# A decoder layer on one core: the last norm's weights on ScalarE, x2 in steps of 704 columns, and four steps moved ahead of others

## The chip, the cores and the metric

One core of a Trainium2 chip runs the whole kernel. The metric is the device time of one execution in microseconds (us). TensorE multiplies, VectorE and ScalarE do elementwise work, GpSimd does additions in SBUF, and SyncE (SP) issues the DMAs.

## The reference

One decoder layer for 1024 prompt tokens and 8 x 4 sample tokens (1056 columns), all in float32. Cut to what this change touches:

```python
def _rms(x, g):
    y = x * lax.rsqrt(jnp.mean(x * x, axis=-1, keepdims=True) + EPS)
    return y * g

a, k_state, v_state = attn_fn(q, k, v)        # sliding window for the prompt, cache for the samples
...
mix = concatenate([a, m]) @ w_out
x = x + _rms(mix, n_mix_post)
f = _rms(x, n_ffn_pre)
f = (silu(f @ w_gate) * (f @ w_up)) @ w_down
x = x + _rms(f, n_ffn_post)                                  # the last norm: weights gn[:, 3, :] in the kernel
x = x + sigmoid(x @ w_ple_gate) * (p @ w_ple)                # the embedding, with its gate
```

## The kernel before

Features lie on the partitions, tokens on the columns. The 1056 tokens are three groups (0, 1, 2) of 352 columns, and a tensor of 1024 features for one group is eight tiles of 128 x 352, kept as two halves of four tiles (128 x 1408). A product in float32 precision is three matmuls: each operand is split into a rounded part and a remainder (`split`: a cast on ScalarE, L164, then a subtraction on VectorE, L165), and `gemm` issues high x high, high x low and low x high, all on L126. Weights come from DRAM by SP into three raw buffers and are split ahead of their use. `weights(j, ahead)` and `need(k, ahead)` do this, as far ahead as their argument says.

A PSUM tile takes one of eight banks (`bank`), handed out in turn; a matmul into a bank waits for the last reader of the tile that had it before.

The stages, in order: the input norm and projection, the pooling mixer, the attention, the output projection with its norms, eleven slabs of the feed-forward part, and the embedding.

*Attention.* The sample queries are done between the prompt's blocks: `dscores`, then `dturned` twice (eight transposes and one more, copied to SBUF by ScalarE, L747 and L750), then `dvalues`, which multiplies the transposed weights with the cached values. The prompt's eight blocks follow in the order 6, 7, 5, 0, 1, 2, 3, 4: while one block is turned and multiplied, the next one's `scores` are computed. `filler` puts output products between them. Masks are multiplied in `turned` on VectorE, L687 and L689. The weights of the output projection come through `weights`, the last of them in `out_proj`.

*Feed-forward.* Gate and up products of groups 0 and 1 go through sums of weights, which GpSimd makes in four additions of 128 x 512 each (L980), after which ScalarE and VectorE split them (`sh`, `sl`). `hid_put` splits the product of the two (L165, `hid`). `down` multiplies `hid` with the down weights and adds each tile of 128 x 352 to `o` in SBUF (L1077).

*Last norm and embedding.* Group 2 is done with its slabs earlier than groups 0 and 1, so its last norm runs under their slabs. `last_down` is `down` and a Square of the finished tile on ScalarE (L779 for the first, L782), which VectorE sums in `acc` (L783). `ple_steps` is the rest of the norm: loads and split of p, loads of the residual into x2, `rstd_steps` (a matmul with ones, the square root on ScalarE, L302, and on VectorE reciprocal, split and two diagonals `dg`, L310, which two matmuls spread over the partitions as r in a PSUM bank), then for each half y times r (L1107) and, tile by tile, x2 plus y times weight (L1111), and `f_operand`, the split of x2 (cast `fh`, remainder `fl`). `ple_out` computes one output tile: the embedding product (pp, 6 matmuls), the gate product (pg, 24 matmuls), the sigmoid (L1155), and the product and the sum on VectorE (L1157, L1159).

`chain` and `turn` interleave such steps with the matmuls: a generator yields its estimated load on VectorE and a delay, and `turn(n)`, called after n matmuls, resumes it when its time has come. The program's order on each engine comes from there and from a scheduler behind it; `behind` keeps group 2's steps in the order of the program.

Of the kernel before, what the change touches and what calls it, by code (L numbers as in the profile page):

```python
# [12 lines left out]
AF = mybir.ActivationFunctionType  # L13
ALU = mybir.AluOpType
AX = mybir.AxisListType

P = 128
D = 1024
KC = D // P
# [6 lines left out]
N = T // G  # L26
NS = (N,) * G
OFF = tuple(N * g for g in range(G + 1))
# [33 lines left out]
def trunk_kernel(  # L62
# [31 lines left out]
    nc = tc.nc  # L94
    te, ve, se, ge = nc.tensor, nc.vector, nc.scalar, nc.gpsimd
# [14 lines left out]
    def act_tile(shape, dt=F32, s="a"):  # L110
        return apool.tile(shape, dt, tag="a", bufs=A_SLOTS, name=nm(s))
# [21 lines left out]
    def tmp(n, s="t", dt=F32):  # L133
        return spool.tile([P, n], dt, tag="tmp", bufs=6, name=nm(s), padded_shape=[P, NX])
# [7 lines left out]
    gn = const([P, 4, KC], gains)  # L142
# [20 lines left out]
    def split(hi, lo, src):  # L163
        fix(se.copy(hi, src))  # L164
        fix(ve.tensor_tensor(lo, src, hi.bitcast(F32), op=ALU.subtract))  # L165
# [23 lines left out]
    def weights(j, ahead=W_PAIRS - 1):  # L189
        for i in range(j, j + ahead + 1):  # L190
            w_split(i)
            w_load(i + 1)
        return pairs[j]
# [10 lines left out]
    WOA, WO = [[], []], [[None] * 4, [None] * 4]  # L204
# [19 lines left out]
    for s, gs in WALK:  # L224
        pairs_of = []
        for i in range(SLAB):
            c = SLAB * s + i
# [48 lines left out]
    def gemm(ps, ops, start=True, stop=True):  # L276

        last = len(ops) - 1
        for i, (wh, wl, xh, xl) in enumerate(ops):
            mm(ps, wh, xh, start=start and i == 0, stop=False)  # L280
            mm(ps, wh, xl, start=False, stop=False)
            mm(ps, wl, xh, start=False, stop=stop and i == last)
# [52 lines left out]
    def bc4(r):  # L335
        return r.unsqueeze(1).to_broadcast([P, 4, r.shape[1]])
# [311 lines left out]
    def scores(b):  # L648


        t = act_tile([P, 8, WIN])
        cur = [bank() for _ in range(2)]
        prv = [bank() for _ in range(2)] if b else None
        for c in range(4):
            for which, at in ((cur, b), (prv, b - 1)):
                if which is None:
                    continue
                for kv in range(2):
                    rows = slice(64 * kv, 64 * kv + 64)
                    mm(  # L660
                        which[kv][:, c * WIN : (c + 1) * WIN],
                        qT[c][rows, b * WIN : (b + 1) * WIN],
                        kT[rows, at * WIN : (at + 1) * WIN],
                        start=True,
                        stop=True,
                    )
        for kv in range(2):
            tk = t[:, 4 * kv : 4 * kv + 4, :]
            if b:
                se.copy(tk, v4(prv[kv]))  # L670
                ve.copy_predicated(tk, m4(0).bitcast(mybir.dt.int32), v4(cur[kv]))  # L671
            else:
                ve.tensor_tensor(tk, v4(cur[kv]), m4(1), op=ALU.add)
            hs = slice(4 * kv, 4 * kv + 4)
            softmax(tk, 4, 0.125, skp[:, hs], nskp[:, hs])
        return t

    def turned(b, t):

        ptc = act_tile([P, 8, WIN])  # L680
        ptp = act_tile([P, 8, WIN]) if b else None
        for kv in range(2):
            ps = bank()
            hs = slice(4 * kv, 4 * kv + 4)
            for c in range(4):
                mt(ps[:, c * P : (c + 1) * P], t[:, 4 * kv + c, :])
            ve.tensor_tensor(ptc[:, hs, :], v4(ps), m4(2), op=ALU.mult)  # L687
            if b:
                ve.tensor_tensor(ptp[:, hs, :], v4(ps), m4(3), op=ALU.mult)  # L689
        return ptc, ptp  # L690
# [62 lines left out]
    def dvalues(pts, o):  # L753

        sides = [slice(64 * kv, 64 * kv + 64) for kv in range(2)]

        def own(a, b):
            return a.rearrange("p (h r) -> p h r", h=4)[:, :, DSEQ * b : DSEQ * (b + 1)]

        for pt, cols in zip(pts, sides):  # L760
            mm(o[cols, :P], vdec[:, cols], pt[: NDEC * DSEQ, 8, :], start=True, stop=False)
        for b in range(NDEC):
            for pt, cols in zip(pts, sides):
                mm(own(o[cols, :P], b), cvt[:, b, cols], own(pt[:, b, :], b), start=False, stop=b == NDEC - 1)
# [12 lines left out]
    def squares_into(acc_g, src, first):  # L777
        if first:
            se.activation(acc_g, src, AF.Square)  # L779
        else:  # L780
            sq = tmp(src.shape[-1], "sq")
            se.activation(sq, src, AF.Square)  # L782
            ve.tensor_tensor(acc_g, acc_g, sq, op=ALU.add)  # L783
# [10 lines left out]
        se.activation(yv, yv, AF.Identity, scale=gn[:, 1, m : m + 1])  # L794

    def out_proj(m, g):
        w = weights(WO[g != 2][m], int(g == 2))
        ps = bank()
        if ys[g][1] is None:
            ys[g][1] = half(g, s="y")  # L800
        gemm(ps[:, : NS[g]], ops8(w, [mixa[g], mixp[g]]))
        se.activation(ys[g][1][:, m - 4, :], ps[:, : NS[g]], AF.Identity, scale=gn[:, 1, m : m + 1])
        squares_into(acc[g], ps[:, : NS[g]], False)
# [9 lines left out]
    def filler(n):  # L813
        for _ in range(n):
            if fill:
                f, *at = fill.pop(0)
                f(*at)
# [4 lines left out]
    t = scores(order[0])  # L822
# [4 lines left out]
    filler(1)  # L827
    pts.append(dturned(td[1]))
    filler(1)
    dvalues(pts, od)  # L830
    put(od, SEQ, NDEC * DSEQ)
    kse = act_tile([P, NDEC, WIN])
# [3 lines left out]
    nc.scalar.dma_start(vs_o, cvt[DSEQ:, :, :])  # L836
    nc.scalar.dma_start(vn_o, vdec)
    for a, b in zip(order, order[1:] + [None]):
        t2 = None if b is None else scores(b)
        filler(1)  # L840
        parts = turned(a, t)
        filler(1)
        values(a, parts)
        t = t2
# [19 lines left out]
    def turn(n):  # L864

        now[0] += n
        for ch in [ch for ch in chains if ch[2]] or list(chains):
            while ch in chains and ch[1] <= now[0]:
                try:
                    load, wait = next(ch[0])  # L870
                except StopIteration:
                    chains.remove(ch)
                    break
                dve[0] = max(dve[0], now[0]) + load / share[0]
                ch[1] = dve[0] + wait
# [46 lines left out]
    def f_operand(src, g):  # L922
        hi, lo = half(g, F32R, "fh"), half(g, F32R, "fl")
        split(hi, lo, src)
        return hi, lo
# [159 lines left out]
    def last_down(n, m, g):  # L1085
        down(n, m, g)
        if m == 0:
            acc3[g] = acc_tile(g)
        squares_into(acc3[g], os_[g][m // 4][:, m % 4, :], m == 0)

    def ple_steps(g):

        pl = half(g, F32R, "pl")
        pls[g] = pl[:, 0:2, :], pl[:, 2:4, :]
        for k in range(2):
            pr = tmp(NS[g], "pr")
            nc.sync.dma_start(pr, p[:, k, OFF[g] : OFF[g + 1]])
            split(pl[:, k, :], pl[:, 2 + k, :], pr)
        x2s[g] = []
        for h in range(2):  # L1100
            x2[g][h] = half(g, s="x2")
            nc.sync.dma_start(x2[g][h], x1d[g][h])
        r = yield from rstd_steps(acc3[g])
        behind = tc.keep_in_program_order if g == 2 else lambda ins: ins
        for h in range(2):
            yh, xh = os_[g][h], x2[g][h]
            behind(ve.tensor_tensor(yh, yh, bc4(r), op=ALU.mult))  # L1107
            for c in range(4):
                k = 4 * h + c
                behind(  # L1110
                    ve.scalar_tensor_tensor(  # L1111
                        xh[:, c, :], yh[:, c, :], gn[:, 3, k : k + 1], xh[:, c, :], op0=ALU.mult, op1=ALU.add
                    )
                )
                if g == 2 and c % 2:
                    yield 6, 0
            yield 12 if g == 2 else 24, 0
            x2s[g].append(f_operand(xh, g))
            yield 10, 0

    END = len(WALK) - 1

# [22 lines left out]
    def ple_out(n, m, g):  # L1145
        ph, pl = pls[g]
        w = WPE[n][m]
        wh, wl = need(w[0])
        cols = slice((m % 4) * P, (m % 4 + 1) * P)
        pp, pg = bank(), bank()  # L1150
        gemm(pp[:, :N], [(wh[:, k, cols], wl[:, k, cols], ph[:, k, :], pl[:, k, :]) for k in range(2)])
        gemm(pg[:, :N], ops8(need(w[1]), x2s[g]))
        turn(30)
        sg = tmp(N, "sg")
        se.activation(sg, pg[:, :N], AF.Sigmoid)  # L1155
        xm = x2[g][m // 4][:, m % 4, :]
        ve.tensor_tensor(sg, sg, pp[:, :N], op=ALU.mult)  # L1157
        yo = tmp(N, "yo")
        ve.tensor_tensor(yo, sg, xm, op=ALU.add)  # L1159
        nc.sync.dma_start(y_o[:, m, OFF[g] : OFF[g + 1]], yo)  # L1160
# [105 lines left out]
```

## Time and profile before

| | |
|---|---|
| median of three runs | 1124.63 us (1122.67 to 1124.66) |
| the profiled execution | 1121.84 us, its span 1120.1 us |
| granted clock of TensorE in the profiled execution | 0.997 |
| VectorE, ScalarE, GpSimd busy | 748.4, 440.7, 179.5 us |
| HBM read and written | 88.30 and 10.11 MB |
| DMA of p (176 KB) and of x2 (704 KB), issue to landing | 2.7 and 6.2 us |

The span is the time from the first to the last instruction in the trace. A time such as 868.51 is counted from its start. PE is TensorE, DVE VectorE, ACT ScalarE, POOL GpSimd. In a row, `out<-in` gives the program's names of the tiles without their numbers, and a line number belongs to the kernel before. Matmuls overlap, so the length of one (0.32 us for 352 columns) is twice the distance to the next.

### The profile page before, as it was taken

To read this page: it belongs to the slowest core of one execution; us is meant where nothing else is said; L and a number is where in the kernel's file an instruction comes from. 1 tells how busy PE (TensorE), PEld (TensorE's weight loads), DVE (VectorE), ACT (ScalarE), POOL (GpSimd) and SP (SyncE) were. 2 spreads that over 40 slices of the span, in tenths; PEclk is the share of its full clock that TensorE was granted. 3 is DMA by queue.
4 is the path that set the end of the run, shared out by engine and by line. 5 is a ranking of instruction groups with operands and counts; after the bars stand their busy time and mean duration, and the time that the engine had idled before them with its cause. 6 is when DMAs were issued, how large, how long until landed. Compare 5 with 4: busy or idle time off the path is not lost.

```text
span 1120.1 us, 17702 instructions
## 1 busy us (share of the span) xinstructions
PE 1108.9 (99%) x7171; PEld 1090.8 (97%) x7171; DVE 748.4 (67%) x1244; ACT 440.7 (39%) x782; POOL 179.5 (16%) x152
## 2 busy tenths in 40 slices
PE   8999999999999999999999999999999999999998
PEld 8999988899999999999999999999999999999998
DVE  6667468985879955355554555557887877789532
ACT  8323276664646524331321314124424334366220
POOL 0045132200000041011111101111132123100000
PEclk9999999999999999999999999999999999999999
DMA  8121311272543312111110212112212222246211
GB/s 288 57 70 43 119 41 38 83 265 71 206 159 132 114 38 76 39 61 54 38 57 20 75 38 76 39 39 93 104 57 77 74 76 79 96 161 215 91 58 39
DMA packets 35265, 99.54 MB, mean 89 GB/s; under 512 B 4180, under 2 KB 14708, under 8 KB 35184
## 3 DMA queue, kind: packets, MB, share of 16 engines
q1 hardware_dynamic: 33856, 96.65, 25.6%
q10 hardware_dynamic: 1328, 1.77, 0.5%
q8 instruction: 56, 0.92, 0.4%
q14 instruction: 25, 0.20, 0.1%
HBM read 88.30 MB, written 10.11 MB: 88 GB/s over the span
## 4 chain that ended last, share of the span: by engine, by line
PE 88%; DVE 6%; ACT 3%; DMA 1%; issue 1%; POOL 0%; SPq 0%; DVEq 0%; ACTq 0%; POOLq 0%
PE b L126 88%; ACT a L634 1%; DVE wl L165 1%; DMA xr<-in_x_dram 1%; DVE mx L626 1%; DVE a L671 1%; ACT wh L164 1%; POOL wr L980 0%; DVE h L366 0%; PE b L120 0%; DMA c<-in_gains_dram 0%; DVE o L1107 0%; DVE x L1111 0%; DVE a L734 0%; DVE p L1014 0%
## 5 line engine op out<-in xcount | busy, mean ns | idle before, releaser
L126 PE MATMUL b<-fh,wh 128*128 128x352 f32 x808 | 260.7, 323 | 0.0
L126 PE MATMUL b<-fh,wl 128*128 128x352 f32 x808 | 259.3, 321 | 0.0
L126 PE MATMUL b<-fl,wh 128*128 128x352 f32 x808 | 259.0, 321 | 0.0
L126 PE MATMUL b<-hid,wh 128*128 128x352 f32 x1056 | 252.5, 322 | 1.7 <-DVE o L1107 1.2
L164 ACT CAST wh<-wr 128x1024 fp32r<-128x1024 f32 (+1 forms) x139 | 142.9, 1030 | 249.6 <-PE b L126 206.6
L165 DVE TENSOR_TENSOR wl<-wr,wh 128x1024 fp32r<-128x1024 f32 (+1 forms) x139 | 171.7, 1238 | 63.8 <-ACT wh L164 63.6
L126 PEld LDWEIGHTS b<-hid,wh 128*128 128x128 f32 x1056 | 182.3, 188 | 2.5 <-issue 1.5
L126 PE MATMUL b<-hid,wl 128*128 128x352 f32 x528 | 169.0, 320 | 0.0
L980 POOL TENSOR_TENSOR wr<-wr 128x512 f32<-128x512 f32 x44 | 63.4, 1441 | 622.3 <-DVE wl L165 451.8
L126 PEld LDWEIGHTS b<-fl,wh 128*128 128x128 f32 x808 | 151.8, 188 | 0.0
L126 PEld LDWEIGHTS b<-fh,wl 128*128 128x128 f32 x808 | 151.8, 188 | 0.0
L126 PEld LDWEIGHTS b<-fh,wh 128*128 128x128 f32 x808 | 151.6, 188 | 0.0
L1077 DVE TENSOR_TENSOR o<-o,b 128x352 f32<-128x352 f32 x240 | 114.7, 514 | 27.3 <-PE b L126 27.2
L126 PE MATMUL b<-fh,sh 128*128 128x352 f32 x352 | 113.6, 323 | 0.0
L126 PE MATMUL b<-fl,sh 128*128 128x352 f32 x352 | 112.8, 320 | 0.0
L126 PE MATMUL b<-fh,sl 128*128 128x352 f32 x352 | 112.7, 320 | 0.0
L126 PE MATMUL b<-h,wh 128*128 128x352 f32 x480 | 106.1, 327 | 1.3 <-ACT h L364 0.9
L165 DVE TENSOR_TENSOR sl<-wr,sh 128x1024 fp32r<-128x1024 f32 x44 | 53.7, 1222 | 75.5 <-ACT sh L164 75.5
L126 PEld LDWEIGHTS b<-hid,wl 128*128 128x128 f32 x528 | 99.0, 187 | 0.0
L164 ACT CAST sh<-wr 128x1024 fp32r<-128x1024 f32 x44 | 45.7, 1047 | 130.9 <-POOL wr L980 91.3
L126 PEld LDWEIGHTS b<-h,wh 128*128 128x128 f32 x480 | 82.6, 190 | 2.6 <-DVE h L366 1.3
L126 PE MATMUL b<-h,wl 128*128 128x352 f32 x240 | 66.3, 325 | 0.0
(150 smaller groups left out, 1593.3 us busy)
## 6 DMA issues: line engine op xcount, KB each, us to landing
wr<-in_w_gu_dram SPq DMA_DIRECT2D x64, 512.0 KB, 3.3
wr<-in_w_dn_dram SPq DMA_DIRECT2D x32, 512.0 KB, 3.5
wr<-in_w_pg_dram SPq DMA_DIRECT2D x14, 512.0 KB, 3.7
x<-in_x_dram SPq DMA_DIRECT2D x6, 704.0 KB, 7.7
x1d<-x SPq DMA_DIRECT2D x6, 704.0 KB, 3.5
x<-x1d SPq DMA_DIRECT2D x6, 704.0 KB, 6.2
out_y_dram<-yo SPq DMA_DIRECT2D x24, 176.0 KB, 1.8
wr<-in_w_out_b_dram SPq DMA_DIRECT2D x8, 512.0 KB, 3.3
```

The lines of the kernel that those rows point to most:

```text
L126: ins = te.matmul(*args, **kw)
L164: fix(se.copy(hi, src))
L165: fix(ve.tensor_tensor(lo, src, hi.bitcast(F32), op=ALU.subtract))
L626: ve.tensor_reduce(mx, t, axis=AX.X, op=ALU.max)
L634: se.activation(t[:, c, :], t[:, c, :], AF.Exp, bias=nmx[:, c : c + 1], scale=scale, accum_out=sm[:, c : c + 1])
L671: ve.copy_predicated(tk, m4(0).bitcast(mybir.dt.int32), v4(cur[kv]))
L980: ge.tensor_tensor(out, a, b, op=op)
L1077: ve.tensor_tensor(o, o, v, op=ALU.add)
```

## The change

Five things are edited. In `last_down` the weight of the last norm is multiplied into the tile by ScalarE (an Identity with a scale, in place, after the Square). In `ple_steps` p comes in one DMA into a buffer of the activation pool, the loads are issued first, y times r and x2 plus y are done in steps of two tiles (704 columns) without the weight, and the split of p comes last. In `ple_out` the gate product is ahead of the embedding product, and the sigmoid is between them. In the attention the scores of the second block are ahead of `dvalues`. For the last block the split of the first weight of the output projection for groups 0 and 1 is called for behind `turned`, and `out_proj` fetches one weight less ahead at its end.

```diff
     def out_proj(m, g):
-        w = weights(WO[g != 2][m], int(g == 2))
+        w = weights(WO[g != 2][m], int(g == 2 and m < KC - 1))
...
     pts.append(dturned(td[1]))
     filler(1)
+    ahead = scores(order[1])
     dvalues(pts, od)
     put(od, SEQ, NDEC * DSEQ)
...
     for a, b in zip(order, order[1:] + [None]):
-        t2 = None if b is None else scores(b)
+        t2 = ahead or (None if b is None else scores(b))
+        ahead = None
         filler(1)
         parts = turned(a, t)
+        if b is None:
+            weights(WOA[1][0], 1)
         filler(1)
...
     def last_down(n, m, g):
-        squares_into(acc3[g], os_[g][m // 4][:, m % 4, :], m == 0)
+        o = os_[g][m // 4][:, m % 4, :]
+        squares_into(acc3[g], o, m == 0)
+        se.activation(o, o, AF.Identity, scale=gn[:, 3, m : m + 1])
 
     def ple_steps(g):
         pl = half(g, F32R, "pl")
         pls[g] = pl[:, 0:2, :], pl[:, 2:4, :]
-        for k in range(2):
-            pr = tmp(NS[g], "pr")
-            nc.sync.dma_start(pr, p[:, k, OFF[g] : OFF[g + 1]])
-            split(pl[:, k, :], pl[:, 2 + k, :], pr)
+        raw = act_tile([P, 2, NS[g]])
+        nc.sync.dma_start(raw, p[:, :, OFF[g] : OFF[g + 1]])
         x2s[g] = []
         for h in range(2):
             x2[g][h] = half(g, s="x2")
             nc.sync.dma_start(x2[g][h], x1d[g][h])
         r = yield from rstd_steps(acc3[g])
         behind = tc.keep_in_program_order if g == 2 else lambda ins: ins
         for h in range(2):
-            yh, xh = os_[g][h], x2[g][h]
-            behind(ve.tensor_tensor(yh, yh, bc4(r), op=ALU.mult))
-            for c in range(4):
-                k = 4 * h + c
-                behind(
-                    ve.scalar_tensor_tensor(
-                        xh[:, c, :], yh[:, c, :], gn[:, 3, k : k + 1], xh[:, c, :], op0=ALU.mult, op1=ALU.add
-                    )
-                )
-                if g == 2 and c % 2:
-                    yield 6, 0
-            yield 12 if g == 2 else 24, 0
-            x2s[g].append(f_operand(xh, g))
+            for c in (0, 2):
+                yc, xc = (t[g][h][:, c : c + 2, :] for t in (os_, x2))
+                behind(ve.tensor_tensor(yc, yc, r.unsqueeze(1).to_broadcast([P, 2, r.shape[1]]), op=ALU.mult))
+                behind(ve.tensor_tensor(xc, xc, yc, op=ALU.add))
+                yield 11, 0
+            x2s[g].append(f_operand(x2[g][h], g))
             yield 10, 0
+        split(*pls[g], raw)
+        yield 6, 0
...
     def ple_out(n, m, g):
         pp, pg = bank(), bank()
-        gemm(pp[:, :N], [(wh[:, k, cols], wl[:, k, cols], ph[:, k, :], pl[:, k, :]) for k in range(2)])
         gemm(pg[:, :N], ops8(need(w[1]), x2s[g]))
-        turn(30)
+        turn(24)
         sg = tmp(N, "sg")
         se.activation(sg, pg[:, :N], AF.Sigmoid)
+        gemm(pp[:, :N], [(wh[:, k, cols], wl[:, k, cols], ph[:, k, :], pl[:, k, :]) for k in range(2)])
+        turn(6)
```

## The prediction, made before the changed kernel was run

> **What bounds the kernel now.** I read the page's busy table first, then the list of waits of TensorE, then the chain of waits for where each one falls, and the timelines around those places.
>
> ```profile
> span 1120.1 us, 17702 instructions
> PE 1108.9 (99%) x7171; PEld 1090.8 (97%) x7171; DVE 748.4 (67%) x1244; ACT 440.7 (39%) x782; POOL 179.5 (16%) x152
> ```
>
> TensorE is busy 99% of the span. The change removes no matmul and adds none, so all it can move is the few microseconds in which TensorE stands still, and the work after its last matmul. The list of TensorE's waits (what was waited for, total, times, longest) names those the change comes near:
>
> ```profile
> PE b L126 <- DVE o L1107: 1.2, 1, 1.2
> PE b L126 <- DVE dg L310: 0.8, 2, 0.4
> PE b L126 <- DVE a L687: 0.7, 2, 0.4
> PE b L126 <- ACT a L750: 0.5, 1, 0.5
> PE b L126 <- DVE hid L165: 0.5, 1, 0.5
> ```
>
> Together 3.7 us. Of the two waits on dg one lies before 140 us, in a norm that is not touched. The chain of waits (start, length, what) shows three of the others and the tail:
>
> ```profile
> 819.21 1.54 DVE hid L165
> 820.80 28.41 PE b L126 x176
> ...
> 864.53 1.06 ACT sh L164
> 865.61 1.22 DVE sl L165
> 866.84 1.54 DVE o L1107
> 868.51 129.75 PE b L126 x815
> ...
> 1003.40 0.45 DVE dg L310
> 1003.89 111.78 PE b L126 x701
> 1115.69 0.47 ACT sg L1155
> 1116.18 0.53 DVE sg L1157
> ```
>
> Between these places TensorE runs 352-column matmuls without a break, 129.75 us for 815, or 0.16 us each. One tile of a down product (6 matmuls) is then 0.96 us, a gate product (24) 3.8 us, an embedding product (6) 0.96 us.
>
> **The change part by part.** The profiled execution took 1121.84 us, 1.74 above its span; the median of the runs is 1124.63, 2.79 above the profiled one. I work out a difference against the profiled execution and put it on both.
>
> *Scores ahead of the sample queries' values.* The timelines of TensorE and of ScalarE at this place:
>
> ```profile
> 147.36 0.43 PE L126 MATMUL b<-a,a 32*64 32x128 f32 x2
> 148.33 2.34 PE L126 MATMUL b<-a,a 32*64 32x128 f32 x46 [0.55 <-ACT a L750]
> 153.75 1.04 PE L120 MATMUL b<-c,a 128*128 128x128 f32 x8
> ```
>
> ```profile
> 146.73 0.44 ACT L773 COPY y<-b 128x352 f32<-128x352 f32 x1
> 147.08 1.04 ACT L747 COPY a<-b 128x512 f32<-128x512 f32 x2
> 148.03 0.25 ACT L750 COPY a<-b 32x128 f32<-32x128 f32 x1
> ```
>
> dvalues starts at 147.36 and stands 0.55 us for the last dturned copy, which ends at 148.28. The change issues the 16 matmuls of the next block's scores first; by the transposes' row (8 in 1.04) they take about 2.1 us. The four PSUM banks they need are released by copies that end no later than 147.17 (the one at 146.73), before dvalues' old start. So dvalues begins near 149.4, after the copy: 0.55 saved. Behind dvalues, its eviction and the sample outputs move 2 us later, and nothing on TensorE waits for them. If a bank came only with the end of the pair of copies at 147.08 (148.12), TensorE would stand 0.76 in place of 0.55, a loss of 0.2. The gain stays only if the waits on L687 at 216 to 224 us start from TensorE's own times. The chain of work in front of them runs back to ScalarE, which had itself stood waiting for TensorE:
>
> ```profile
> 177.88 1.08 ACT L670 COPY a<-b 128x512 f32<-128x512 f32 x2 [1.31 <-PE b L126]
> ```
>
> It idled 1.31 us there, so with matmuls 0.55 earlier this chain and the waits at its end shift along.
>
> *Last masks ahead of splits.* In the built order the split of that weight still stands ahead of the masks L687 on VectorE, and ScalarE and SP keep their order there too. This part does nothing: the 0.7 us on L687 stay.
>
> *Group 2's x2 in steps of 704.* VectorE's timeline before 820.80, and the GpSimd row beside it:
>
> ```profile
> 814.09 1.61 DVE L1107 TENSOR_TENSOR o<-o,b 128x1408 f32<-128x1408 f32 x1
> 816.06 3.15 DVE L1111 SCALAR_TENSOR_TENSOR x<-o,c,x 128x352 f32<-128x352 f32 x2
> 819.13 1.61 DVE L165 TENSOR_TENSOR hid<-u,hid 128x352 fp32r<-128x352 f32 x1
> ```
>
> ```profile
> 815.68 3.14 POOL L980 TENSOR_TENSOR wr<-wr,wr 128x512 f32<-128x512 f32 x2
> ```
>
> ```profile
> L1111 DVE SCALAR_TENSOR_TENSOR x<-o,c,x x24: 549/574/1616, 816.1 to 1042.0; 128x352 f32<-128x352 f32 x24
> ```
>
> The weighted adds take 1.57 us each while GpSimd's sums run, against 0.55 to 0.57 elsewhere; L1107, which reads PSUM for one input, takes its usual 1.61. The Trainium skill (GPSIMD Engine Reference, Specifications) states that GpSimd shares its SBUF interfaces with VectorE, in contention where VectorE has two SBUF inputs; the rows agree, and by it the new 704-column adds would be held too. The new order in front of hid is y 704, u, x 704. y of half the columns is half of 1.61, 0.8. For the add the nearest rows bound it: 0.8 if it runs free, 3.14 if it is held as two 352-column ones are; I take 1.6 to 1.9, one hold, since the held operations end with a GpSimd sum whatever they are. From 814.09: 0.8, u 0.44, 1.9, hid 1.6 gives 818.8; with 3.14 it is 820.0. TensorE is ready 0.5 before 820.80. So 0.5 of 0.5 is saved, 0.2 at the worst end.
>
> The rest of that half's x2 moves to about 836, and half 1's to about 878 and 893, so VectorE goes from the split sl straight to evictions. At 868.51 TensorE waited for a PSUM bank that holds group 2's broadcast r, last read by L1107. In the new program that matmul takes another bank, freed by a 352-column eviction right behind sl: sl ends at 866.83, an eviction is about 0.5, and TensorE starts 0.13 after VectorE's end as it did at 868.51 (866.84 + 1.54 = 868.38): 867.45, against 868.51. That saves 1.1; with another VectorE piece of 0.8 between them 0.3.
>
> *Gate ahead of embedding.* At the end the sigmoid (1115.69) now runs under the 0.96 us of pp, and VectorE's product starts when pp ends, where the sigmoid started: 1116.18 less 1115.69, 0.49 saved. Each x2 operand is needed 0.96 us earlier; group 1's two pl splits now stand behind it and give VectorE more than that.
>
> *Weights on ScalarE, and group 0's rstd.* This is the part that can cost.
>
> ```profile
> 986.89 1.05 ACT L164 CAST wh<-wr 128x1024 fp32r<-128x1024 f32 x1 [1.49 <-PE b L126]
> 987.96 1.28 ACT L1155 ACT_TABLE_LOAD   x1
> 989.66 0.50 ACT L779 ACTIVATE acc<-o 128x352 f32<-128x352 f32 x1
> 998.28 1.05 ACT L164 CAST wh<-wr 128x1024 fp32r<-128x1024 f32 x1 [0.69 <-PE b L126]
> 999.24 0.49 ACT L782 ACTIVATE sq<-o 128x352 f32<-128x352 f32 x1
> 1001.04 0.26 ACT L302 ACTIVATE sd<-b,c 88x4 f32<-88x4 f32 x1
> ```
>
> ```profile
> 231.25 0.48 ACT L779 ACTIVATE acc<-y 128x352 f32<-128x352 f32 x1
> 231.77 0.59 ACT L794 ACTIVATE y<-y,c 128x352 f32<-128x352 f32 x1
> ```
>
> ```profile
> 1002.88 0.52 DVE L165 TENSOR_TENSOR pl<-pr,pl 128x352 fp32r<-128x352 f32 x1
> 1003.31 0.52 DVE L310 TENSOR_TENSOR dg<-c,hl 88x352 fp32r<-88x352 f32 x1
> ```
>
> Each down tile now has a Square and, waiting for it, an Identity: the pair at 231.25 shows 0.52 from start to start and 0.59 for the second; a row of ScalarE that waits for nothing starts about 0.1 before the one ahead of it ends (999.24 against 998.28 + 1.05). That is 1.03 a pair. TensorE makes a tile in 0.96, so ScalarE is the slower of the two. It also starts earlier: the cast at 986.89 waited for the gate product, which is now 0.96 sooner, so the first Square is at 988.7. Ten pairs bring it to 999.0; cast 1.05, Square 0.4, table load 1.3: sqrt at 1001.8, 0.75 later than 1001.04. Behind it, VectorE no longer has the two pl splits (0.43 from start to start, one ahead of each dg), but an eviction now falls there: second dg done at 1004.1 instead of 1003.83, TensorE on at 1004.2 instead of 1003.89. A loss of 0.3; with pairs of 0.96 a gain of 0.4, and with no overlap (1.12 a pair) a loss of 1.2.
>
> The Trainium skill's ScalarE: Activation LUTs, Rules for kernel authors, speaks against this: it sends multiplies to VectorE. Its price for the Identity (186 + 93 + 0.833 x 352) is 572 ns, an estimate from that page, and the trace's 0.59 agrees; by its rule the pairs are too dear, which is the first rival below.
>
> *Loads first.* On SP's queue the p and x2 loads of group 2 pass four weight loads; they wait for matmuls that end before those that the passed loads wait for, so nothing is held. Group 0's p and first x2 go ahead of one w_dn load and the second x2 ahead of one w_pg load, also behind waits that end earlier; what can grow is that load's time to landing, and its weight is cast several microseconds ahead of its first matmul. Nothing; with that cover gone, the microseconds by which it lands late. p now goes to one buffer of its own size and its split comes last, behind the x2 operands, where only pp of group 0 and 1 waits for it.
>
> Sum: 0.55 + 0.5 + 1.1 + 0.49 - 0.3 = 2.3 us less. Profiled execution 1119.5; median 1122.3.
>
> **The rivals.**
> 1. *ScalarE is the late engine at the end.* Pairs of 1.12 cost 1.2 at 1003.89 in place of 0.3: a gain of 1.4, 1123.2. For it: 1.03 is already above 0.96. Against: the overlap of 0.1 at 999.24.
> 2. *The attention's 0.55 is given back* at the masks (216 to 224), if their chain hangs on VectorE's total work rather than on the matmul at 177.90: a gain of 1.8, 1122.8. Against: ScalarE's idle 1.31 at 177.88.
> 3. *Slower: adds of 704 held by GpSimd for their columns.* If a hold is 3.14 per add, 820 gains 0.2 and the pieces at 836, 878 and 893 each cost 2.3 more (3.14 less 0.8). It decides where a hold exceeds what VectorE is ahead of TensorE by, for which I take 1.2, the size of its longest wait. Two of the three on TensorE's path, less that margin each, are 2.3; with the eviction at 867 lost as well, and 0.55 + 0.49 + 0.2 - 0.3 kept, the time is 1.4 more, 1126.0; with all three on the path 2.5 more, 1127.1. For it: two 352-column adds took 3.15. Against: those were two holds.
> 4. *More:* ScalarE keeps up with TensorE (pairs of 0.96), group 0's rstd comes 0.4 earlier, and the wait of 1.2 at 868.51 goes whole: 0.55 + 0.5 + 1.2 + 0.49 + 0.4 is 3.1 less, 1121.5. For it: its cast starts 0.96 sooner. Against: rival 1's rows.
> That a part does nothing is already in the sum, for the masks.
>
> **How the numbers follow.** Forecast 0.45 (own range 1121.6 to 1123.0), rival 1 0.15, rival 2 0.11, rival 3 0.13, rival 4 0.16. 0.2% is 2.25 us, about what a measurement of this kernel can tell from no change: below 1122.4 is faster, above 1126.9 slower. Of the forecast 0.30 lies below; with rival 4 and 0.04 from executions that differ by more than a microsecond (the three runs span 2.0) that is 0.50 faster. Slower takes 0.09 of rival 3 (all three pieces) and 0.05 for runs that fall above the median of before: 0.14. Same: 0.36. The range goes from 1119.7 (rival 4, less most of the 2.0 that the runs span) to 1126.0, rival 3 with two holds; beyond lie its worse half and executions out of the way, 0.2 together.
>
> **What would show it.** Right: no wait on ACT a L750 at 148; no wait of TensorE on the new y line; hid no longer waited for at 820; a wait on dg near 1003 of 0.5 to 1.2; the last sigmoid done before pp; the waits on L687 unchanged at 0.7. Wrong: a new wait of TensorE on an eviction between 836 and 915, adds of 704 at 3 us, or the sqrt at 1003 or later.

## The result, and the profile after

The changed kernel takes 1127.33 us (median of 7 runs, 1125.46 to 1128.71) against 1123.05 us for the kernel before (7 runs, 1122.11 to 1124.66): a ratio of 1.0034, 95% interval 1.0022 to 1.0046. It is slower by about 4.3 us; 2.3 us less had been forecast, and the time lies above the range given. Its profiled execution took 1128.71 us, 1126.9 of them span (before 1121.84 and 1120.1).

The head of the page of the changed kernel: span, and busy time by engine.

```profile
span 1126.9 us, 17700 instructions
PE 1110.7 (99%) x7171; PEld 1092.5 (97%) x7171; DVE 748.1 (66%) x1235; ACT 451.7 (40%) x803; POOL 182.1 (16%) x152
```

The matmuls are the same in number, TensorE is busy 1.8 us longer, and VectorE is not busier. So some matmuls took longer, and the rest of the 6.8 us by which the span grew is new standing. The list of what TensorE waited for (total, times, longest), in the changed kernel:

```profile
PE b L126 <- ACT hid L164: 3.7, 1, 3.7
PE b L126 <- DVE dg L310: 2.8, 2, 1.7
PE b L126 <- DVE o L1081: 0.8, 1, 0.8
PE b L126 <- DVE a L687: 0.7, 2, 0.4
PE b L126 <- DVE hid L165: 0.6, 1, 0.6
```

The first row is new and as large as the five named before together. The waits on L750 and on y times r (L1107) are gone. The wait on hid of 0.6 is not the one of before at 819.21: it stands behind the new one. The chain of waits of the changed kernel (start, length, what), at the places shown of before:

```profile
224.38 599.10 PE b L126 x3792
...
866.97 0.44 DVE o L1081
867.46 6.81 PE b L126 x41
...
906.36 1.27 POOL wr L984
907.65 1.05 ACT sh L164
908.73 1.22 DVE sl L165
909.95 0.45 DVE hid L165
910.44 57.23 PE b L126 x343
...
983.09 7.28 DMA wr<-in_w_dn_dram
990.44 1.06 ACT wh L164
...
1011.68 111.09 PE b L126 x701
1122.86 0.53 DVE sg L1157
1123.42 0.52 DVE yo L1159
```

TensorE runs through 820 without a break, and at 867 it goes on behind an eviction of 0.44 instead of y times r of 1.54: both as forecast. But at 910.44 stands a chain that did not exist: GpSimd's sums, a cast sh, its remainder sl, and only then the remainder of hid. Where the matmuls of the two executions stand against each other shows the size of each place (worked out from the starts of the matmuls in the two traces, numbered from the first):

| matmul | at (before), us | changed kernel, start less that of before |
|---|---|---|
| 300 | 53.5 | +0.60 |
| 1050, behind the attention's first blocks | 160.2 | -0.32 |
| 5320, ahead of 820 | 818.4 | +0.03 |
| 5600, behind 820 | 863.8 | -0.64 |
| 5900, behind 867 and 905 | 912.9 | +6.60 |
| 6470, behind the wait on dg | 1003.9 | +7.79 |
| 7170, the last | 1115.3 | +7.11 |

Nearly the whole loss, 7.2 us net and 7.6 with what 867 gained, comes between the matmuls 5600 and 5900; 1.2 more comes at dg. The +0.60 at matmul 300 lies ahead of every edited step; there the profiled executions of the other kernels differ from before by -0.45 to +0.53.

**The place at 905.** ScalarE's timeline, before and then in the changed kernel (start, length, operation, and in brackets how long it stood and for whom):

```profile
902.68 0.49 ACT L164 CAST hid<-u 128x352 fp32r<-128x352 f32 x1 [0.77 <-DVE u L1058]
904.71 0.50 ACT L1026 ACTIVATE c<-c 128x352 f32<-128x352 f32 x1 [1.54 <-DVE c L1014]
908.11 1.05 ACT L164 CAST sh<-wr 128x1024 fp32r<-128x1024 f32 x1 [2.91 <-POOL wr L980]
```

```profile
903.42 0.50 ACT L1030 ACTIVATE c<-c 128x352 f32<-128x352 f32 x1
907.65 1.04 ACT L164 CAST sh<-wr 128x1024 fp32r<-128x1024 f32 x1 [3.74 <-POOL wr L984]
908.60 0.48 ACT L164 CAST hid<-u 128x352 fp32r<-128x352 f32 x1
```

Before, the cast of hid from u came ahead of c and sh. Now it stands behind both, and in front of it sh waits 3.74 us for GpSimd. The cast of hid waits with it: its input u is done at 905.15, and the cast starts at 908.60, right behind sh. VectorE, first one row of before and then the changed kernel, and TensorE in the changed kernel:

```profile
902.13 0.52 DVE L1058 TENSOR_TENSOR u<-u,p 128x352 f32<-128x352 f32 x1
```

```profile
893.89 0.88 DVE L1113 TENSOR_TENSOR x<-x,o 128x704 f32<-128x704 f32 x1
896.22 1.62 DVE L165 TENSOR_TENSOR fl<-x,fh 128x1408 fp32r<-128x1408 f32 x1 [0.38 <-ACT fh L164]
903.52 1.63 DVE L1062 TENSOR_TENSOR u<-u,p 128x352 f32<-128x352 f32 x1
```

```profile
905.07 0.32 PE L126 MATMUL b<-hid,wl 128*128 128x352 f32 x1
909.14 0.66 PE L126 MATMUL b<-hid,wh 128*128 128x352 f32 x1 [3.75 <-ACT hid L164]
910.44 0.66 PE L126 MATMUL b<-hid,wh 128*128 128x352 f32 x1 [0.65 <-DVE hid L165]
```

The split of group 2's second half (fh, fl) now falls into this slab: fl is at 896.22, where before it started at 891.83. Behind it, u times p comes at 903.52 instead of 902.13, and so starts inside GpSimd's sums (902.10 to 907.6), where it takes 1.63 instead of 0.52. That alone would have delayed hid little: u ends at 905.15, its cast 0.5 later, and TensorE would have stood about half a microsecond (an estimate from these rows). With the place in ScalarE's queue it stands 3.9 us, and for the remainder hid, on VectorE behind sl, 1.15 more: together 5.05 us. It then does not return at full speed. Its windows (start:end, length, busy time and count of PE, PEld, DVE, ACT, POOL, then granted clock, DMA share, GB/s):

```profile
895.00:905.00 10.00, 10.00 (x65) 10.00 (x64) 9.30 (x13) 4.85 (x7) 2.74 (x3) 1.00 0.32 106
905.00:910.40 5.40, 1.05 (x4) 0.39 (x2) 2.68 (x6) 1.43 (x2) 2.54 (x2) 0.87 0.00 0
910.40:915.70 5.30, 5.26 (x18) 5.26 (x19) 2.41 (x5) 0.00 (x0) 0.00 (x0) 0.50 0.32 99
915.70:925.00 9.30, 9.30 (x60) 9.30 (x59) 6.43 (x12) 2.88 (x3) 0.00 (x0) 0.99 0.19 58
```

For 5.3 us the granted clock is 0.50, and about 20 matmuls take 0.29 us each instead of 0.16: 2.55 us more. 5.05 and 2.55 are the 7.6. With them the 4.3 us by which the medians differ come out: the kernel with the delay, below, is 3.1 faster than before, and 7.6 less 3.1 is 4.5.

### The profile page after: what moved, and what is told of

Its sections match the earlier page's. It is cut to its first block, busy times and chain, and to the rows that moved or that the text cites. A ratio compares the mean times of both kernels' runs of the same rounds, so it can differ in the third digit from the quotient of the medians.

```text
span 1126.9 us, 17700 instructions
## 1 busy us (share of the span) xinstructions
PE 1110.7 (99%) x7171; PEld 1092.5 (97%) x7171; DVE 748.1 (66%) x1235; ACT 451.7 (40%) x803; POOL 182.1 (16%) x152
## 4 chain that ended last, share of the span: by engine, by line
PE 81%; DVE 7%; ACT 4%; POOL 3%; DMA 2%; issue 2%; POOLq 0%; SPq 0%; DVEq 0%; ACTq 0%
PE b L126 81%; POOL wr L984 2%; DVE wl L165 2%; ACT wh L164 1%; DMA xr<-in_x_dram 1%; DMA a<-in_dmask_dram 1%; ACT a L634 1%; DVE mx L626 1%; DMA wr<-in_w_dn_dram 1%; DVE sl L165 1%; DVE a L671 1%; ACT sh L164 0%; PE b L120 0%; ACT sq L782 0%; ACT o L1095 0%
```

## The experiments

The theory: the loss is the place of hid's cast in ScalarE's queue, behind a cast that waits for GpSimd, which the split of group 2's second half brings about by falling into that slab; the half clock follows from the standing. The rivals: that the end loses it (Identities on ScalarE, loads first), or that group 2's weights on ScalarE and its steps of 704 lose it by themselves, in whatever order.

### The split of the second half, 20 units later

```diff
                 yield 11, 0
+            if g == 2 and h:
+                yield 20, 0
             x2s[g].append(f_operand(x2[g][h], g))
```

> The changed kernel with one more yield of 20 ahead of group 2's second f_operand: the split of x2 comes one slab later, and on ScalarE the cast of hid is again ahead of the casts sh. Theory A (the 5 us at 905 and the half clock behind it are one cast of hid standing behind sh, which waits for GpSimd): both go, some 7.5 us, to about 1119.8. Rival B (the adds of 704 columns held by GpSimd make VectorE late as such): the stall only moves with the split, 1126 to 1128. Rival C (the loss is at the end, in the late w_dn weight and in ScalarE's pairs): 1127.

Measured 1119.37 us, a ratio to before of 0.9969 (0.9957 to 0.9982), span 1117.6. One delay and nothing else turns the loss of 4.3 us into a gain of 3. fl now starts at 931.77 instead of 896.22. ScalarE's timeline at the same place:

```profile
900.89 0.49 ACT L164 CAST hid<-u 128x352 fp32r<-128x352 f32 x1 [0.73 <-DVE u L1062]
902.92 0.50 ACT L1030 ACTIVATE c<-c 128x352 f32<-128x352 f32 x1 [1.54 <-DVE c L1018]
906.32 1.05 ACT L164 CAST sh<-wr 128x1024 fp32r<-128x1024 f32 x1 [2.90 <-POOL wr L984]
```

The order of before is back, hid's cast ahead of sh. Its chain of waits has no break in that stretch, and the window in which the changed kernel stood is full at full clock:

```profile
866.64 131.56 PE b L126 x830
```

```profile
905.00:910.40 5.40, 5.40 (x36) 5.40 (x35) 3.00 (x6) 2.10 (x2) 1.29 (x1) 1.00 0.12 33
```

### Group 2's last norm as before, the rest changed

```diff
-        se.activation(o, o, AF.Identity, scale=gn[:, 3, m : m + 1])
+        if not (g == 2):
+            se.activation(o, o, AF.Identity, scale=gn[:, 3, m : m + 1])
...
+            if g == 2:
+                yh, xh = os_[g][h], x2[g][h]
+                behind(ve.tensor_tensor(yh, yh, bc4(r), op=ALU.mult))
+                for c in range(4):
+                    k = 4 * h + c
...
```

> The changed kernel with group 2's last norm as before (weight in VectorE's adds, y in 1408, x2 in tiles); all else changed. Theory A: no stall at 905, but the waits at 820 and 867 are back (1.0 us together): about 1120.8. Rival C: no better than 1126, since nothing at the end is touched.

1120.91 us, ratio 0.9985 (0.9976 to 0.9995). The standing at 905 and the half clock are gone, and the waits at 820 and 867 are back (0.73 and 1.19 from start to start). Both belong to group 2's part; the loss does not belong to the end.

### Groups 0 and 1: loads and split of p as before, the rest changed

```diff
-        raw = act_tile([P, 2, NS[g]])
-        nc.sync.dma_start(raw, p[:, :, OFF[g] : OFF[g + 1]])
+        if g == 2:
+            raw = act_tile([P, 2, NS[g]])
+            nc.sync.dma_start(raw, p[:, :, OFF[g] : OFF[g + 1]])
+        else:
+            for k in range(2):
+                pr = tmp(NS[g], "pr")
+                nc.sync.dma_start(pr, p[:, k, OFF[g] : OFF[g + 1]])
+                split(pl[:, k, :], pl[:, 2 + k, :], pr)
...
-        split(*pls[g], raw)
-        yield 6, 0
+        if g == 2:
+            split(*pls[g], raw)
+            yield 6, 0
```

> The changed kernel with the loads and the split of p of groups 0 and 1 as before; group 2's stay changed. The w_dn weight no longer shares its time with 1 MB of other loads. Theory A: the stall at 905 stays, and of the 2.2 us at the dg matmuls about 1 goes: 1126.3. Rival C: 1123 to 1124.

1127.36 us, ratio 1.0041 (1.0026 to 1.0056): still slow, with the same standing (5.07 us) and the same half clock (2.77 us more). The wait on dg fell from 2.18 to 1.69, half of what was expected. So the loads of groups 0 and 1 are not the cause.

### The kernel before with group 2's part alone

```diff
+        if g == 2:
+            se.activation(o, o, AF.Identity, scale=gn[:, 3, m : m + 1])
...
+            if g == 2:
+                for c in (0, 2):
+                    yc, xc = (t[g][h][:, c : c + 2, :] for t in (os_, x2))
+                    behind(ve.tensor_tensor(yc, yc, r.unsqueeze(1).to_broadcast([P, 2, r.shape[1]]), op=ALU.mult))
+                    behind(ve.tensor_tensor(xc, xc, yc, op=ALU.add))
+                    yield 11, 0
```

> The kernel before with group 2's weights on ScalarE and x2 in steps of 704 and nothing else. Its ScalarE order has the cast of hid behind sh as the changed kernel has. Theory A: 1.0 saved at 820 and 867, 7.5 lost at 905: about 1129.5. Rival C: 1122.

1130.61 us, ratio 1.0065 (1.005 to 1.008): this part alone brings the whole loss at 905, 7.9 us between the same matmuls as above. Its time is above that of the whole change, which has gains elsewhere; and its profiled execution loses 1.65 us more at 150 us, in a stage that this kernel has as before (last section). Its waits of TensorE, its ScalarE at the place, and the window behind it:

```profile
PE b L126 <- ACT hid L164: 3.8, 1, 3.8
PE b L126 <- DVE hid L165: 0.9, 1, 0.9
```

```profile
909.07 1.04 ACT L164 CAST sh<-wr 128x1024 fp32r<-128x1024 f32 x1 [3.75 <-POOL wr L980]
910.02 0.48 ACT L164 CAST hid<-u 128x352 fp32r<-128x352 f32 x1
```

```profile
912.00:917.00 5.00, 5.00 (x17) 5.00 (x18) 2.23 (x5) 0.00 (x0) 0.00 (x0) 0.50 0.32 105
```

### Group 2's part alone, with the split 20 units later

The edit is to the kernel of the run above, group 2's part alone:

```diff
+            if g == 2 and h:
+                yield 20, 0
             x2s[g].append(f_operand(x2[g][h], g))
```

> The kernel before with group 2's weights on ScalarE, x2 in steps of 704, and the yield of 20 ahead of its second f_operand. Against the run with group 2's part alone only the place of that split differs. Theory A: 7.6 us less than that run, and below the kernel before by what the waits at 820 and 867 give together, about 1.1 (the prediction had 1.6 for the two). Rival B: slower than the kernel before.

1121.51 us, ratio 0.9993 (0.9984 to 1.0002): 9.1 us less than without the delay, 7.6 of them at this place in the two traces. The weights are on ScalarE and the steps are 704 columns in both, so neither makes the loss by itself; it comes with the place of the split, and with the order that this brings about. The wait at 820 is gone here as well, and the one at 867 is 0.95 instead of 1.37 from start to start.

### Longer steps instead of a delay

```diff
-                yield 11, 0
+                yield (16 if g == 2 else 11), 0
```

> The changed kernel with group 2's x2 steps yielding 16 in place of 11: another way to the same order on ScalarE (the cast of hid ahead of sh in every slab), with the adds of 704 columns at other places. Theory A: about 3 below the kernel before, no stall at 905. Rival B: adds held at other places give stalls there, no better than the kernel before.

1120.0 us, ratio 0.998 (0.997 to 0.999), span 1116.7. Another edit that moves the same piece; hid's cast (899.44) is again ahead of sh (904.87), and of the standing 0.4 us is left, behind an eviction at 907.66. No run exchanges the two casts and nothing else: in every kernel without the loss the split stands elsewhere as well (fl at 890 to 893 or at 931 to 934, and at 894 to 898 in the three with the loss). That the place in the queue makes most of the loss, and not the late u, is read from the trace of the changed kernel, where hid's cast starts 3.45 us after u is done.

### The attention's part alone

```diff
+    ahead = scores(order[1])
     dvalues(pts, od)
...
-        t2 = None if b is None else scores(b)
+        t2 = ahead or (None if b is None else scores(b))
+        ahead = None
```

> The kernel before with the scores of the second block ahead of dvalues and nothing else. The prediction's step: the 0.55 us at 148 goes and stays gone: 0.55 below the kernel before. Rival: the masks at 216 to 224 take it back: same as before, with waits on L687 of 1.2 in place of 0.7.

1122.09 us against 1124.27, ratio 0.9983 (0.9973 to 0.9994). In the traces the matmuls behind the attention start 1.1 us earlier than before, down to the last one; as this execution was 0.36 late ahead of dvalues, the part gives 1.45, more than twice the forecast. The wait on L750 is gone and that on L687 is 0.7 as before.

### The gate ahead of the embedding alone

```diff
-        gemm(pp[:, :N], [(wh[:, k, cols], wl[:, k, cols], ph[:, k, :], pl[:, k, :]) for k in range(2)])
         gemm(pg[:, :N], ops8(need(w[1]), x2s[g]))
-        turn(30)
+        turn(24)
         se.activation(sg, pg[:, :N], AF.Sigmoid)
+        gemm(pp[:, :N], [(wh[:, k, cols], wl[:, k, cols], ph[:, k, :], pl[:, k, :]) for k in range(2)])
+        turn(6)
```

> The kernel before with the gate product ahead of the embedding product and nothing else. The prediction's step: 0.4 to 0.5 below the kernel before, all of it behind the last matmul. Rival: x2 and the weights, needed 0.96 us earlier, make TensorE wait for as much: same.

1123.3 us, ratio 0.9997 (0.9988 to 1.0006): no difference that can be told. The end behind the last matmul is 0.42 shorter, but the wait on dg grows from 0.99 to 1.69. VectorE's timeline there:

```profile
1001.55 0.17 DVE L303 RECIPROCAL sd<-sd 88x4 f32<-88x4 f32 x1
1002.05 0.95 DVE L165 TENSOR_TENSOR pl<-pr,pl 128x352 fp32r<-128x352 f32 x2
1003.50 0.95 DVE L310 TENSOR_TENSOR dg<-c,hl 88x352 fp32r<-88x352 f32 x2
```

The two splits of p stand between the reciprocal and dg. In the whole change they come last, so this part and the late split belong together.

### Loads first and the late split alone

```diff
-        for k in range(2):
-            pr = tmp(NS[g], "pr")
-            nc.sync.dma_start(pr, p[:, k, OFF[g] : OFF[g + 1]])
-            split(pl[:, k, :], pl[:, 2 + k, :], pr)
+        raw = act_tile([P, 2, NS[g]])
+        nc.sync.dma_start(raw, p[:, :, OFF[g] : OFF[g + 1]])
...
+        split(*pls[g], raw)
+        yield 6, 0
```

> The kernel before with p in one load ahead of x2 and its split behind the x2 operands, nothing else. The two splits leave VectorE in front of the diagonals: the dg wait falls from 1.0 to about 0.4; and if the pace of 158.2 ns per matmul at the end comes from this part, 0.7 more: 1.2 below the kernel before together. Rival: the w_dn weight lands late behind 1 MB: same or slower, with ScalarE waiting for it at 982.

1123.92 us, ratio 1.0009 (1.0001 to 1.0018). From start to start the wait on dg falls by 0.39, and a new one appears, because pp, still ahead of the gate here, needs the split that now comes last:

```profile
PE b L126 <- DVE pl L165: 1.4, 1, 1.4
```

### Groups 0 and 1: weights on ScalarE and steps of 704, alone

```diff
+        if g != 2:
+            se.activation(o, o, AF.Identity, scale=gn[:, 3, m : m + 1])
...
+            if g != 2:
+                for c in (0, 2):
+                    yc, xc = (t[g][h][:, c : c + 2, :] for t in (os_, x2))
...
```

> The kernel before with the weights on ScalarE and steps of 704 for groups 0 and 1 only. ScalarE starts no earlier here (the gate is behind pp), so with pairs of 1.01 the square root of group 0 comes some 1.5 later: the wait at the dg matmuls grows from 1.0 to 2 to 2.5, 1.0 to 1.5 slower than the kernel before. Rival: VectorE's lighter x2 gives it back: same.

1124.06 us, ratio 1.0014 (1.0005 to 1.0024). The wait on dg is 1.99 instead of 0.99. ScalarE reaches the square root at 1001.58 instead of 1001.04, and VectorE, which has evictions and a split of p to do behind it, reaches dg at 1003.95 instead of 1002.44. The square root is 0.5 late and not 1.5: here ScalarE does two Squares and then two Identities, at 0.87 a tile (990.75 to 992.48 for two), and not pairs of 1.01.

### The delayed kernel, with the end's parts undone

Both edits are to the kernel with the split 20 units later. First, groups 0 and 1 with their last norm as before:

```diff
-        se.activation(o, o, AF.Identity, scale=gn[:, 3, m : m + 1])
+        if not (g != 2):
+            se.activation(o, o, AF.Identity, scale=gn[:, 3, m : m + 1])
...
+            if g != 2:
+                yh, xh = os_[g][h], x2[g][h]
+                behind(ve.tensor_tensor(yh, yh, bc4(r), op=ALU.mult))
+                for c in range(4):
+                    k = 4 * h + c
...
```

> As the run with the split one slab later, but groups 0 and 1 have their last norm as before (weight in VectorE's adds); the loads, the split of p and the order of the gate stay changed. If ScalarE's pairs of Square and Identity are what makes the square root of group 0 late, the wait at the dg matmuls falls from 1.3 to 0.3 or less: about 1118.4. Rival: VectorE, with five operations per half again, becomes late for x2 instead: 1119.4 or more.

1120.08 us, ratio 0.9966 (0.9953 to 0.9979), against 0.9969 with the pairs: the two cannot be told apart. In the traces the wait on dg is 0.79 instead of 1.26, so the pairs of Square and Identity cost 0.47 there. In this kernel's trace that gain is hidden: its 560 matmuls between the matmuls 5900 and 6460 take 160.0 ns each instead of 157.8, 1.2 us more, with no wait listed (last section).

Then, groups 0 and 1 with loads and split of p as before:

```diff
-        raw = act_tile([P, 2, NS[g]])
-        nc.sync.dma_start(raw, p[:, :, OFF[g] : OFF[g + 1]])
+        if g == 2:
+            raw = act_tile([P, 2, NS[g]])
+            nc.sync.dma_start(raw, p[:, :, OFF[g] : OFF[g + 1]])
+        else:
+            for k in range(2):
...
```

> As the run with the split one slab later, but the loads and the split of p of groups 0 and 1 are as before. With two splits of p ahead of the diagonals again and, as the run with these loads alone undone showed, 160.0 in place of 158.9 ns per matmul at the end (0.7 us): 1120.5. Rival: the 1 MB ahead of the w_dn weight is what costs: 1118.5.

1120.99 us, ratio 0.9975 (0.9966 to 0.9984). The wait on dg is 1.69 instead of 1.26: once the gate is ahead, the late split is worth 0.43. The intervals of this kernel and of the delayed one overlap.

The lowest ratios of all the kernels that ran are those of the changed one with the delay (0.9969) and of the same with the end's norm as before (0.9966).

## Why the prediction was wrong, step by step

**The step that failed** is in the part on steps of 704: "The rest of that half's x2 moves to about 836, and half 1's to about 878 and 893, so VectorE goes from the split sl straight to evictions." The pieces did land there (878.49 and 893.89). But they were followed on VectorE alone, and only as far as 867. Behind the piece at 893 comes f_operand, fh on ScalarE and fl on VectorE, which thereby entered the slab that ends at 905; nobody asked what that slab had room for, nor what stood behind what on ScalarE. ScalarE's rows show the exchange: hid's cast ahead of c and sh before, behind both of them after. The prediction compares the engines' orders for the masks, and not in this slab. The list of signs that would make the prediction wrong (an eviction between 836 and 915, held adds, a late square root) named the right stretch and no wait on ScalarE in it.

The terms of the sum, against the kernel with the delay, in which nothing covers them (differences of starts in the traces, one execution each):

| term | forecast | measured |
|---|---|---|
| attention | 0.55 less | 1.45 less (1.45 to 1.47 in every trace that has this part) |
| masks | nothing | nothing: 0.7 on L687 in all |
| 820 and 867 | 1.6 less | 1.1 less |
| 905 | not in the sum | nothing with the delay, 7.6 more without |
| group 0's rstd | 0.3 more | 0.27 more; 1.2 more in the changed kernel's profile |
| gate ahead, at the end | 0.49 less | 0.43 less |
| pace of the last 700 matmuls | not in the sum | 0.68 less |

*Attention.* The mechanism was right, the size not. The 0.55 is idle time behind the modelled end of two short matmuls. From the start of dvalues to the next product it is 147.36 to 151.72 before, 4.36, and in the changed kernel

```profile
148.49 3.46 PE L126 MATMUL b<-a,a 64*128 64x128 f32 x68
151.88 0.43 PE L126 MATMUL b<-mh,wh 128*128 128x352 f32 x1
```

3.39: 0.97 saved. A wait should be priced from start to start. Another 0.48 was gained where neither the list nor the prediction has a wait: from the first block's product with its values to the next product it is 4.07 before (156.63 to 160.70) and 3.59 in the changed kernel. Before, two of these matmuls start 0.05 to 0.06 behind masks that VectorE ends at 157.06 and 157.75; in the changed kernel, with the scores earlier, the masks end 0.6 earlier. The scores are 32 matmuls and not the 16 of the prediction, and take 1.98 us (148.49 to 150.47): the 2.1 taken for them was near by luck.

*820 and 867.* The wait at 820 went, worth 0.67 from start to start. In the changed kernel hid was done at 819.5 and not at 818.8, since u, taken at 0.44, was held too and took 1.10, but TensorE came to it only at 820.1. The saving at 867 was right by itself, and the two were added although they overlap. The sum at 867 assumed that sl would end where it did, at 866.83, while TensorE came earlier by what 820 gave. With the delay sl starts at 864.93, 0.68 earlier than before, a little less than TensorE had gained ahead of 820 (0.80); the chain of sums and casts did not follow the further 0.67 that TensorE gained at 820. So 867 gave 0.4 and not 1.1.

*Group 0's rstd.* The pairs run at 1.01, against 1.03 forecast, and ScalarE is the slower engine as said (changed kernel):

```profile
997.98 0.59 ACT L1095 ACTIVATE o<-o,c 128x352 f32<-128x352 f32 x1
998.99 0.59 ACT L1095 ACTIVATE o<-o,c 128x352 f32<-128x352 f32 x1
```

Where the wait is 1.26 instead of 0.99 the forecast 0.3 holds. In the changed kernel's profile the wait is 2.18: the load of w_dn took 7.28 us to land there (983.09 in the chain), so its cast, the table load and the first Square came late. The prediction had put this at nothing and named the price if the cover went, "the microseconds by which it lands late"; 0.9 of them counted.

*The rivals.* Rival 1 (ScalarE late at the end) did not happen in the size given; rival 2 did not happen. Rival 3 had the sign, by another mechanism. Of the twelve adds of 704 one was held:

```profile
L1113 DVE TENSOR_TENSOR x<-x,o x12: 856/881/1978, 816.0 to 1047.4; 128x704 f32<-128x704 f32 x12
```

1.98 us for that one, at 816.0 beside GpSimd's sums, near the 1.6 to 1.9 taken, and 0.88 for the median; none took 3 us. Rival 4 did not happen: the pairs were not down to 0.96, and 0.95 us of the standing at 867 stayed. The kernel with the delay gains 3.1 us by its median, 2.4 without the pace, against 2.3 forecast. That this is so near is in part luck: the attention gave 0.9 more than forecast and 820 and 867 together 0.5 less. What the sum left out decided.

## What to carry to other kernels

Where an edit moves a piece of work into another stage, follow every operation that the piece issues, on every engine's queue, to the end of that stage: an operation of half a microsecond that is planned behind one that waits for a slow engine costs that engine's time. Compare the built orders of the engines side by side, look for two operations exchanged, and ask what the one in front waits for. Then price the standing from start to start, and add the matmuls that run at half clock behind it if it lasts several microseconds.

## What the runs showed of the hardware

- After 5.05 to 5.07 us of standing TensorE ran at a granted clock of 0.50 for about 5.3 us, in all three kernels that stood there: 2.6 to 2.8 us on top of the standing. After the 2.2 us at dg in the changed kernel there was no such loss:

```profile
1009.00:1011.70 2.70, 0.94 (x6) 0.42 (x4) 2.39 (x9) 2.69 (x7) 0.00 (x0) 1.00 0.57 194
1011.70:1017.00 5.30, 5.30 (x33) 5.30 (x34) 5.30 (x9) 4.92 (x11) 0.00 (x0) 1.00 0.00 0
```

  The Trainium skill (TensorE: Matmul & The Clock Gate, Why this matters for your kernels) advises against gaps of more than about 3 us between matmuls, since one idle window brings the clock back to half; the places at 905 and at dg agree with it, 5.05 and 2.2. One place does not: in the profiled execution of group 2's part alone the clock fell to 0.50 at 149.7 for 3.4 us, with 0.56 us of standing ahead of it (148.2), and 1.65 us were lost; the kernel before stood 0.55 there and kept its full clock. So in these traces a short standing is not always without this loss. The prediction did not weigh the rule, as it saw no gap of that length.
- u times p took 1.63 us where it started just behind the start of one of GpSimd's sums (903.52, the sum at 903.48), 1.10 where it started in the middle of one (814.98), and 0.52 where it started ahead of the first (902.13 before, the sum at 902.35). One add of 704 columns took 1.98 against 0.88. So a VectorE operation that slips by a microsecond into such a stretch can lose another.
- The 700 matmuls of the end run at 158.2 ns each in the changed kernel and some of the others, and at 159.2 ns in the kernel before and the rest, 0.7 us in all. It goes with no single part of the change (the kernels with groups 0 and 1's norm on ScalarE alone, with the late split alone, and with the delay and the end's norm undone have the faster pace, the ones with the attention or group 2 alone the slower). Its cause stays open; where the tiles lie was not tried. The 560 matmuls from 5900 on show the same: 157.8 ns each in the kernel before and most others, 158.9 in three (group 2's norm as before, and group 2's part alone with and without the delay), 160.0 in the one with the delay and the end's norm undone. A difference of a microsecond between two kernels can come from this alone.
